# A three-stack transformer kernel: columns for the first norm's weights, halves for the first unit and for the output, products of zeros at the start

## The chip, the cores and the metric

The kernel runs on one core of one Trainium2 chip. A core has five engines with instruction queues of their own: TensorE (PE) for matrix products, VectorE (DVE), ScalarE (ACT), GpSimd (POOL), and SyncE (SP), which here issues DMA transfers. The metric is device time in microseconds for one execution, the median of several runs; before the change it is 2333.55 us (three runs, 2333.11 to 2333.55).

## The reference

The input is 512 tokens of width 1024 in float32. Two hybrid layers follow (dilated attention, mLSTM, gated mixing, a feed-forward part), a norm, then a second block of two layers (latent attention and gated linear attention, with a context of 256 tokens) and a last norm. What the change touches is the first operation and the last two:

```
def rms_norm(x, w):
    xf = x.astype(jnp.float32)
    y = xf * lax.rsqrt(jnp.mean(xf * xf, axis=-1, keepdims=True) + NORM_EPS)
    return (y * w.astype(jnp.float32)).astype(x.dtype)

h = rms_norm(x, norm_mix_w)      # first layer: the first thing that is computed
z = h @ w_in + b_in              # the first columns of z are the queries
...
x = x + gx * yx                  # second block, second layer: the last projection
return rms_norm(x, final_g)      # the output, (1, 512, 1024)
```

## The kernel before, in words

Tokens lie in four tiles of 128 partitions, `xs[0]` to `xs[3]`, each 128x1024. Weights come from memory in units of 128x1024 (512 KB) in the order in which they are used; `P.stream` gives a function `W` that hands out the next unit. A product in float32 is made of three products in the faster type float32r: every operand `v` is held as a high part (`v` rounded, made by ACT, line 251) and a low part (`v` less its high part, made by DVE, line 252). `split` makes the two, `mm3` (lines 280 to 282) issues high by high, high by low and low by high into one PSUM bank. `wide_acc` does eight steps of `mm3` for one token tile over four units: 24 products with 512 columns.

At the start SP issues, in this order, tile x0, the identity, the norm's weights `wbc` (one row of 4 KB repeated over 128 partitions, line 221), units 0 and 1, x1, units 2 and 3, x2, x3, and then small tables. `Norm` takes one tile at a time: ACT squares it with a running sum (line 298), DVE makes the mean (289), POOL the power -1/2 (291), DVE multiplies by that number and by the row of weights in one pass (300), PE transposes the eight 128x128 blocks into two PSUM banks (757), and each bank is split by one ACT and one DVE instruction into `big`, the stationary operand of the products. Between tile 0 and tile 1 the program asks for the first four units, so their splits stand there. The Q projection then runs over the four tiles (line 414 adds the bias and frees the bank), followed by K, V and the rest.

The unit's raw landing place has two slots (four for the first units, in `land`), the split unit has four. A slot is loaded again when its split is done, and a split unit is overwritten when the products that read it are done.

At the end `output(1)` of `gla` goes through tiles and, for each, two halves `ch` of 512 columns: 12 products, DVE times the gate (1574), DVE adds to `xs[t]` (1575). After the second half `rms` squares the whole tile on ACT, makes the mean and the power, scales it in one DVE pass of 1024 columns (300), and SP stores 512 KB (1578). Two PSUM banks `A` take turns there.

The order of instructions on each engine is settled when the kernel is built: a planner goes through the program with its own estimates of durations and gives each engine, whenever it is free, the earliest instruction in program order that is ready by them. On the chip each engine keeps that order. Lines 973 and 974, in another class (`Tokens.put`), split transposed blocks one by one with a number per partition, much as the changed kernel does in its first norm.

Of the kernel before, what the change touches and what calls it, by code (L numbers as in the profile page):

```python
# [25 lines left out]
C_AQ, C_AK, C_AV, C_MQ, C_MK, C_MV, C_MO = (512 * i for i in range(7))  # L26
C_MI = 3584
C_GA, C_GB = 3592, 4616
QUARTERS = ((0, 0), (0, 1), (1, 1), (1, 0))


# [13 lines left out]
def _cols(v):  # L45

    return v.reshape(-1, 128).T
# [116 lines left out]
def layout(a):  # L164
    m = {}
    for l in range(2):
        m[f"wl{l}"] = pack_layer(a, l)
        m[f"wq{l}"] = pack_quarters(a, l)
        m[f"cl{l}"] = pack_cols(a, l)
        m[f"wg{l}"] = np.ascontiguousarray(_tall(a["w_in"][l], C_MI, 8))  # L170
    m["x"] = a["x"].reshape(S, D)
    m["pos"] = np.ascontiguousarray(a["positions"].reshape(4, 128).T)
    for k in ("b_in", "norm_mix_w", "norm_mlp_w"):
        m[k] = a[k]
    m["mla"], m["gla"], m["gla_g"] = pack_mla(a), pack_gla(a), pack_gates(a)
    m["gla_b"] = np.concatenate([_cols(a["gla_b_gb_2"][0]), _cols(a["gla_b_gf_2"][0])], axis=1)
    m["gla_o_norm"] = a["gla_o_norm_2"]
    m["mla_q_norm"], m["mla_kv_norm"] = a["mla_q_norm_2"], a["mla_kv_norm_2"]
    for i in range(2):
        m[f"ada{i}"] = a["ada_w_2"][i].T.reshape(24, 128, 1024)  # L180
    m["ada_b"] = np.stack([_cols(a["ada_b_2"][i]) for i in range(2)], axis=1)
    m["cvec"] = np.concatenate([a["c_2"].reshape(-1), a["c_ctx_2"].reshape(-1)])
    m["norm_g"] = np.stack([_cols(a["norm_g_2"][i]) for i in range(2)])
    m["final_g"] = a["final_g_2"].reshape(1, D)
    m["ctx"] = a["ctx_2"].reshape(256, D)
    m["final_norm_w"] = a["final_norm_w"].reshape(1, D)
    m.update({"k_" + k: v for k, v in constants().items()})
    return {k: np.ascontiguousarray(v) for k, v in m.items()}
# [8 lines left out]
class Prog:  # L197
# [59 lines left out]
    def stream(self, key):  # L257
        units = self.A[key]
        state = {"i": 0}
        ahead = []  # L260

        def fetch(n=1024, raw=None):
            raw = self.raw.tile([128, 1024], F32, name="raw") if raw is None else raw
            self.nc.sync.dma_start(raw[:, 0:n], units[state["i"]][:, 0:n])
            state["i"] += 1
            ahead.append(raw)

        def nxt(n=1024):
            if not ahead:
                fetch(n)  # L270
            raw = ahead.pop(0)
            w = self.spl.tile([128, 2, 1024], F32R, name="spl")
            self.split(w[:, 0, 0:n], w[:, 1, 0:n], raw[:, 0:n])
            return w
        nxt.state, nxt.fetch = state, fetch
        return nxt
# [26 lines left out]
def act_of(tiles):  # L303

    return lambda k: (tiles[k // 4][:, 0, k % 4], tiles[k // 4][:, 1, k % 4])


def cut(a):

    return lambda t, k: tuple(v[:, t * 128:(t + 1) * 128] for v in a(k))  # L310
# [31 lines left out]
def first_block(P, xs, pool):  # L342
# [6 lines left out]
    for l in range(2):  # L349
# [9 lines left out]
        if l == 0:  # L359
            def load_x(t):  # L360
                nc.sync.dma_start(xs[t], A["x"][t * 128:(t + 1) * 128])
            load_x(0)
            P.ident = P.load(P.const, "k_ident", [128, 128], "ident")
            norm = Norm(P, xs, A["norm_mix_w"][0], one, tmp, big)
            land = big(3, F32).rearrange("p a k n -> p (a k n)").rearrange("p (i n) -> p i n", i=4)
            for i in (0, 1):
                W.fetch(raw=land[:, i])
            load_x(1)
            for i in (2, 3):
                W.fetch(raw=land[:, i])  # L370
            for t in (2, 3):
                load_x(t)
            for t in range(4):
                norm(t)()
                if t == 0:
                    first += [W() for _ in range(4)]
            mod = Modulation(P)
            dil = P.load(ck, "k_dil", [128, 512], "dil")
            anti = P.load(ck, "k_anti", [128, 128], "anti")
            pair = P.load(ck, "k_pair", [128, 5], "pair")  # L380
            pair_r = ck.tile([128, 4], F32R, name="pair_r")
            nc.scalar.activation(pair_r, pair[:, 0:4], AF.Copy)
# [356 lines left out]
class Norm:  # L739
# [7 lines left out]
    def __call__(self, t):  # L747

        P = self.P
        xn = self.tmp.tile([128, 1024], F32, name="xn", tag="qm")  # L750
        rms(P, xn, self.xs[t], self.wbc, xn)

        def later():
            for g in range(2):
                ps = P.bankT()
                for k in range(4):
                    P.nc.tensor.transpose(ps[:, k * 128:(k + 1) * 128], xn[:, (4 * g + k) * 128:(4 * g + k + 1) * 128],
                                          P.ident)
                o = slice(t * 128, (t + 1) * 128)
                P.split(self.dst[g][:, 0, :, o], self.dst[g][:, 1, :, o], ps.rearrange("p (k n) -> p k n", k=4))  # L760
        return later


# [538 lines left out]
def gla(P, xs, finish, keep, mod, out):  # L1302
# [246 lines left out]
    def output(kh):  # L1549
        sg = gate[0]  # L1550
        if kh == 0:
            output.G = right.tile([128, 1024], F32, name="G", tag="qk0")
            gate_row(P, output.G, mod, 0)
        G = output.G
        oT = left.tile([128, 2, 4, 512], F32R, name="oT", tag=f"hx{kh}")
        for h in (2 * kh, 2 * kh + 1):
            v = sg[:, :, h * 256:(h + 1) * 256]
            nc.vector.tensor_tensor(v, v, held[h], op=OP.mult)
        for t in range(4):
            ps = P.bankT()  # L1560
            for k in range(4):
                nc.tensor.transpose(ps[:, k * 128:(k + 1) * 128], sg[:, t, (4 * kh + k) * 128:(4 * kh + k + 1) * 128], P.ident)
            d = oT[:, :, :, t * 128:(t + 1) * 128]
            P.split(d[:, 0], d[:, 1], ps.rearrange("p (k n) -> p k n", k=4))
        yield
        a, us = cut(act_of([oT])), {}
        order = [(ch, t) for ch in range(2) for t in range(4)]
        for ch, t in [(ch, t) for t in range(4) for ch in range(2)] if kh else order:
            if ch not in us:
                us[ch] = [W() for _ in range(2)]  # L1570
            c = slice(ch * 512, (ch + 1) * 512)
            ps = P.bankA()
            wide_acc(P, ps, us[ch], a, t, 4)
            nc.vector.tensor_tensor(ps, ps, G[:, c], op=OP.mult)
            nc.vector.tensor_tensor(xs[t][:, c], xs[t][:, c], ps, op=OP.add)
            if kh and ch:
                rms(P, xs[t], xs[t], row, right.tile([128, 1024], F32, name="sq", tag=f"qk{2 + t % 2}"))
                nc.sync.dma_start(out[t * 128:(t + 1) * 128], xs[t])
            yield


# [38 lines left out]
```

## Time and profile before

| what | value |
|---|---|
| median of three runs | 2333.55 us |
| the profiled execution's own time | 2335.07 us |
| its span, first to last instruction | 2333.3 us |
| PE busy | 2284.1 us, 98% |
| DVE busy | 1478.0 us, 63% |
| ACT busy | 1063.0 us, 46% |
| granted clock of PE, mean | 0.998 |

All times in rows are microseconds from the span's start unless marked ns. `PE` is the product, `PEld` the load of its stationary operand, which overlaps the product before. An idle time in brackets is that of the engine just before the row, with what ended it. A matrix product's duration covers its way through the array, so the spacing of the starts, or the chain of waits, tells what one costs in a run of them.

### The profile page before, as it was taken

The numbers are of one execution on the slowest core, as the hardware profiler recorded it, in microseconds if no ns is written. First come the engines' busy times: TensorE is split into PE (matmuls) and PEld (weight loads), VectorE is DVE, ScalarE is ACT, GpSimd is POOL, SyncE is SP. The second block draws the span as 40 slices with busy tenths as digits, with TensorE's granted clock in tenths as the row PEclk, the third lists the DMA queues.
The fourth block names the chain that finished last, engine by engine and source line by source line (L and its number), as shares of the span: only waits on it lengthen the run. The fifth ranks groups of instructions, "written<-read, shape, count | busy, mean of one in ns | idle before, by whom it ended". The sixth has DMA issues, their size and how long they took to land.

```text
span 2333.3 us, 30784 instructions
## 1 busy us (share of the span) xinstructions
PE 2284.1 (98%) x12108; PEld 1875.9 (80%) x12108; DVE 1478.0 (63%) x2556; ACT 1063.0 (46%) x1958; POOL 71.4 (3%) x120
## 2 busy tenths in 40 slices
PE   8999999999999999999999999999999999999998
PEld 6777878888888777788888888888888888788886
DVE  4477796555555547779645556564478776756586
ACT  3366423444443235642344445452477772563332
POOL 0000000000000000000000000010000000000000
PEclk9999999999999999999999999999999999999999
DMA  4221464555642322146454554212110121121112
GB/s 162 81 73 55 145 212 142 167 130 151 174 100 91 92 81 75 52 155 216 135 172 120 160 164 116 92 54 72 49 31 21 24 74 37 54 81 37 55 46 72
DMA packets 61312, 234.38 MB, mean 100 GB/s; under 512 B 8544, under 2 KB 9840, under 8 KB 54768
## 3 DMA queue, kind: packets, MB, share of 16 engines
q1 hardware_dynamic: 50512, 179.99, 23.3%
q0 software_dynamic: 3456, 25.17, 6.0%
q10 hardware_dynamic: 7200, 27.27, 3.7%
q8 instruction: 95, 1.56, 0.3%
q14 instruction: 49, 0.40, 0.1%
HBM read 227.15 MB, written 2.10 MB: 98 GB/s over the span
## 4 chain that ended last, share of the span: by engine, by line
PE 81%; DVE 10%; ACT 3%; DMA 3%; issue 2%; POOL 1%; SPq 0%; POOLq 0%; ACTq 0%; DVEq 0%
PE A L282 18%; PE A L281 18%; PE A L280 18%; PE S L280 4%; PE S L282 4%; PE S L281 4%; PE O L1244 2%; DVE spl L252 2%; PE T L1236 2%; PE O L522 1%; DMA ada<-in_ada 1%; PE S L496 1%; DVE junk L933 1%; PE T L516 1%; ACT spl L251 1%
## 5 line engine op out<-in xcount | busy, mean ns | idle before, releaser
L280 PE MATMUL A<-big,spl 128*128 128x512 f32 (+1 forms) x1280 | 482.2, 377 | 1.9 <-DVE x L768 1.2
L282 PE MATMUL A<-big,spl 128*128 128x512 f32 (+1 forms) x1280 | 481.0, 376 | 0.2 <-DVE spl L252 0.2
L281 PE MATMUL A<-big,spl 128*128 128x512 f32 (+1 forms) x1280 | 480.1, 375 | 0.0
L252 DVE TENSOR_TENSOR spl<-raw,spl 128x1024 fp32r<-128x1024 f32 (+2 forms) x265 | 317.2, 1200 | 184.0 <-ACT spl L251 182.2
L251 ACT ACTIVATE spl<-raw 128x1024 fp32r<-128x1024 f32 (+2 forms) x265 | 275.2, 1040 | 292.2 <-PE A L282 190.6
L282 PEld LDWEIGHTS A<-big,spl 128*128 128x128 f32 x1280 | 241.2, 188 | 44.6 <-issue 2.6
L280 PEld LDWEIGHTS A<-big,spl 128*128 128x128 f32 x1280 | 241.3, 189 | 43.9 <-DVE x L768 1.6
L281 PEld LDWEIGHTS A<-big,spl 128*128 128x128 f32 x1280 | 241.3, 189 | 42.5 <-issue 1.4
L252 DVE TENSOR_TENSOR spl<-quarter,spl 128x1024 fp32r<-128x1024 f32 x84 | 102.2, 1223 | 144.9 <-ACT spl L251 144.9
L280 PE MATMUL A<-spl,big 128*128 128x512 f32 (+2 forms) x480 | 182.7, 384 | 3.7 <-DVE tg L668 2.1
L281 PE MATMUL A<-spl,big 128*128 128x512 f32 (+2 forms) x480 | 182.3, 381 | 1.4 <-DVE spl L252 0.8
L282 PE MATMUL A<-spl,big 128*128 128x512 f32 (+2 forms) x480 | 181.7, 380 | 0.2 <-DVE ms L289 0.2
L251 ACT ACTIVATE spl<-quarter 128x1024 fp32r<-128x1024 f32 x84 | 88.2, 1057 | 97.4 <-PE S L282 41.1
L280 PEld LDWEIGHTS A<-spl,big 128*128 128x128 f32 x480 | 90.2, 189 | 23.2 <-DVE tg L668 3.0
L281 PEld LDWEIGHTS A<-spl,big 128*128 128x128 f32 x480 | 90.7, 189 | 18.9 <-DVE spl L252 3.4
L282 PEld LDWEIGHTS A<-spl,big 128*128 128x128 f32 x480 | 90.6, 189 | 16.7 <-issue 1.1
L280 PE MATMUL S<-spl,part 128*128 128x512 f32 x264 | 102.8, 389 | 0.0
L281 PE MATMUL S<-spl,part 128*128 128x512 f32 x264 | 102.8, 389 | 0.0
L282 PE MATMUL S<-spl,part 128*128 128x512 f32 x264 | 102.8, 389 | 0.0
L1211 DVE TENSOR_REDUCE mx<-S 128x1 f32<-128x768 f32 (+1 forms) x80 | 71.8, 900 | 26.5 <-PE S L282 25.7
L291 POOL TENSOR_TENSOR rstd<-ms,mhalf 128x1 f32<-128x1 f32 (+2 forms) x68 | 44.2, 650 | 1247.5 <-DVE ms L289 1203.2
L1237 ACT ACTIVATE pt<-T 128x512 f32<-128x512 f32 (+1 forms) x144 | 66.4, 501 | 32.4 <-PE T L1236 31.2
(442 smaller groups left out, 4349.2 us busy)
## 6 DMA issues: line engine op xcount, KB each, us to landing
raw<-in_wl SPq DMA_DIRECT2D x196, 512.0 KB, 3.7
ada<-in_ada ACTq DMA_DIRECT2D x48, 512.0 KB, 4.0
quarter<-in_wq SPq DMA_DIRECT2D x24, 1024.0 KB, 6.2
quarter<-in_wq POOLq DMA_DIRECT2D x24, 1024.0 KB, 8.7
raw<-in_gla SPq DMA_DIRECT2D x33, 512.0 KB, 3.4
raw<-in_mla SPq DMA_DIRECT2D x20, 512.0 KB, 3.5
raw<-in_mla SPq DMA_DIRECT2D x8, 384.0 KB, 3.0
qT<-rot SPq DMA_DIRECT2D x32, 96.0 KB, 2.8
```

What stands on the lines that cost most here:

```text
L251: nc.scalar.activation(hi, src, AF.Copy)
L252: nc.vector.tensor_tensor(lo, src, f32(hi), op=OP.subtract)
L280: mm(ps, lh, rh, start=start, stop=False, **more)
L281: mm(ps, lh, rl, start=False, stop=False, **more)
L282: mm(ps, ll, rh, start=False, stop=stop, **more)
L291: nc.gpsimd.tensor_tensor(r, ms, self.mhalf[:, 0:w], op=OP.pow)
L496: nc.tensor.matmul(banks[hh][:, 0:w], qT[hs, i, q], kT[hs, j, 0:w], start=(i + j == 0), stop=(i == 1))
L516: nc.tensor.transpose(psp[:, k * 128:(k + 1) * 128], p[:, k * 128:(k + 1) * 128], P.ident)
L1211: nc.vector.tensor_reduce(mx[:, 0:two], pss[:, 0:two * m].rearrange("p (t n) -> p t n", t=two), AX.X, OP.max, negate=True)
L1236: nc.tensor.transpose(pst[:, k:k + 128], p[:, o + k:o + k + 128], P.ident)
L1237: nc.scalar.activation(pt[:, o:o + w], pst[:, 0:w], AF.Copy)
L1244: nc.tensor.matmul(weigh.o[64 * i:64 * i + 64, (t0 + t) * 128:(t0 + t + 1) * 128], V[4 * c + k][:, h * 64:(h + 1) * 64], pts[i][:, t * m + ...
```

## The change

Four edits. (1) The weights of the first layer's first norm are laid out as 128x8 columns, `first_w` (4 KB), and a new class `FirstNorm` takes the place of `Norm` there: DVE multiplies the tile by its number alone, and the weight of each transposed block of 128 features is applied in the split, as the scale of ACT's copy and of DVE's pass, eight of each per tile. (2) Unit 0 is loaded in two transfers of 256 KB and split in two halves. (3) A tile of zeros and 14 products of it (128x128 by 128x512) into one PSUM bank stand ahead of the first norm; nothing reads their result. (4) In the last stage the tile's square is taken in two halves as they are finished, the mean is put together in two DVE steps, and the scaled tile is made and stored in two halves.

```
--- before.py
+++ after.py
@@ -26,6 +26,7 @@
 C_AQ, C_AK, C_AV, C_MQ, C_MK, C_MV, C_MO = (512 * i for i in range(7))
 C_MI = 3584
 C_GA, C_GB = 3592, 4616
+WARM = 14
 QUARTERS = ((0, 0), (0, 1), (1, 1), (1, 0))
 
 
@@ -169,6 +170,7 @@
         m[f"cl{l}"] = pack_cols(a, l)
         m[f"wg{l}"] = np.ascontiguousarray(_tall(a["w_in"][l], C_MI, 8))
     m["x"] = a["x"].reshape(S, D)
+    m["first_w"] = np.ascontiguousarray(_cols(a["norm_mix_w"][0]))
     m["pos"] = np.ascontiguousarray(a["positions"].reshape(4, 128).T)
     for k in ("b_in", "norm_mix_w", "norm_mlp_w"):
         m[k] = a[k]
@@ -259,18 +261,21 @@
         state = {"i": 0}
         ahead = []
 
-        def fetch(n=1024, raw=None):
+        def fetch(n=1024, raw=None, cut=1):
             raw = self.raw.tile([128, 1024], F32, name="raw") if raw is None else raw
-            self.nc.sync.dma_start(raw[:, 0:n], units[state["i"]][:, 0:n])
+            for o in range(0, n, n // cut):
+                self.nc.sync.dma_start(raw[:, o:o + n // cut], units[state["i"]][:, o:o + n // cut])
             state["i"] += 1
             ahead.append(raw)
 
-        def nxt(n=1024):
+        def nxt(n=1024, cut=1):
             if not ahead:
                 fetch(n)
             raw = ahead.pop(0)
             w = self.spl.tile([128, 2, 1024], F32R, name="spl")
-            self.split(w[:, 0, 0:n], w[:, 1, 0:n], raw[:, 0:n])
+            for o in range(0, n, n // cut):
+                c = slice(o, o + n // cut)
+                self.split(w[:, 0, c], w[:, 1, c], raw[:, c])
             return w
         nxt.state, nxt.fetch = state, fetch
         return nxt
@@ -361,19 +366,25 @@
                 nc.sync.dma_start(xs[t], A["x"][t * 128:(t + 1) * 128])
             load_x(0)
             P.ident = P.load(P.const, "k_ident", [128, 128], "ident")
-            norm = Norm(P, xs, A["norm_mix_w"][0], one, tmp, big)
+            norm = FirstNorm(P, xs, one, tmp, big)
             land = big(3, F32).rearrange("p a k n -> p (a k n)").rearrange("p (i n) -> p i n", i=4)
             for i in (0, 1):
-                W.fetch(raw=land[:, i])
+                W.fetch(raw=land[:, i], cut=2 - i)
             load_x(1)
             for i in (2, 3):
                 W.fetch(raw=land[:, i])
             for t in (2, 3):
                 load_x(t)
+
+            nil = tmp.tile([128, 512], F32R, name="nil", tag="yf")
+            nc.vector.tensor_copy(nil, P.zero.to_broadcast([128, 512]))
+            idle = P.bankO()
+            for i in range(WARM):
+                nc.tensor.matmul(idle, nil[:, 0:128], nil, start=(i == 0), stop=(i == WARM - 1))
             for t in range(4):
                 norm(t)()
                 if t == 0:
-                    first += [W() for _ in range(4)]
+                    first += [W(cut=2 - (i > 0)) for i in range(4)]
             mod = Modulation(P)
             dil = P.load(ck, "k_dil", [128, 512], "dil")
             anti = P.load(ck, "k_anti", [128, 128], "anti")
@@ -761,6 +772,35 @@
         return later
 
 
+class FirstNorm:
+
+
+    def __init__(self, P, xs, one, tmp, big):
+        self.col = P.load(one, "first_w", [128, 8], "first_w")
+        self.dst = [big(i) for i in range(2)]
+        self.P, self.xs, self.tmp = P, xs, tmp
+
+    def __call__(self, t):
+        P, nc = self.P, self.P.nc
+        xn = self.tmp.tile([128, 1024], F32, name="xn", tag="qm")
+        ssq = P.sm.tile([128, 1], F32, name="ssq")
+        nc.scalar.activation(xn, self.xs[t], AF.Square, accum_out=ssq)
+        r = P.rstd(ssq, D)
+        nc.vector.tensor_scalar(xn, self.xs[t], r, None, op0=OP.mult)
+
+        def later():
+            o = slice(t * 128, (t + 1) * 128)
+            for g in range(2):
+                ps = P.bankT()
+                for k in range(4):
+                    v, c = ps[:, k * 128:(k + 1) * 128], 4 * g + k
+                    nc.tensor.transpose(v, xn[:, c * 128:(c + 1) * 128], P.ident)
+                for k in range(4):
+                    v, c = ps[:, k * 128:(k + 1) * 128], 4 * g + k
+                    P.split(self.dst[g][:, 0, k, o], self.dst[g][:, 1, k, o], v, scale=self.col[:, c:c + 1])
+        return later
+
+
 def add_wide(P, W, a, xs, scale, done=None):
 
     def evac(ch, t, ps):
@@ -1564,6 +1604,9 @@
             P.split(d[:, 0], d[:, 1], ps.rearrange("p (k n) -> p k n", k=4))
         yield
         a, us = cut(act_of([oT])), {}
+        if kh:
+            eps = P.sm.tile([128, 1], F32, name="eps")
+            nc.gpsimd.memset(eps, EPS)
         order = [(ch, t) for ch in range(2) for t in range(4)]
         for ch, t in [(ch, t) for t in range(4) for ch in range(2)] if kh else order:
             if ch not in us:
@@ -1573,9 +1616,22 @@
             wide_acc(P, ps, us[ch], a, t, 4)
             nc.vector.tensor_tensor(ps, ps, G[:, c], op=OP.mult)
             nc.vector.tensor_tensor(xs[t][:, c], xs[t][:, c], ps, op=OP.add)
-            if kh and ch:
-                rms(P, xs[t], xs[t], row, right.tile([128, 1024], F32, name="sq", tag=f"qk{2 + t % 2}"))
-                nc.sync.dma_start(out[t * 128:(t + 1) * 128], xs[t])
+            if kh:
+
+                if not ch:
+                    sq = right.tile([128, 1024], F32, name="sq", tag=f"qk{2 + t % 2}")
+                ssq = P.sm.tile([128, 1], F32, name="ssq")
+                nc.scalar.activation(sq[:, c], xs[t][:, c], AF.Square, accum_out=ssq)
+                ms = P.sm.tile([128, 1], F32, name="ms")
+                nc.vector.scalar_tensor_tensor(ms, ssq, 1.0 / D, part if ch else eps, op0=OP.mult, op1=OP.add)
+                part = ms
+                if ch:
+                    r = P.sm.tile([128, 1], F32, name="rstd")
+                    nc.gpsimd.tensor_tensor(r, ms, P.mhalf[:, 0:1], op=OP.pow)
+                    for i in range(2):
+                        h = slice(512 * i, 512 * i + 512)
+                        nc.vector.scalar_tensor_tensor(xs[t][:, h], xs[t][:, h], r, row[:, h], op0=OP.mult, op1=OP.mult)
+                        nc.sync.dma_start(out[t * 128:(t + 1) * 128, h], xs[t][:, h])
             yield
 
 
```

## Rows read from the trace of the kernel before

**Rows 1.** The page, section 1: busy time, share of the span, instructions.

```profile
PE 2284.1 (98%) x12108; PEld 1875.9 (80%) x12108; DVE 1478.0 (63%) x2556; ACT 1063.0 (46%) x1958; POOL 71.4 (3%) x120
```

**Rows 2.** Waits of the first 60 us: who waited for whom, total, times, longest.

```profile
ACT spl L251 <- DMA big<-in_wl: 4.7, 2, 4.5
...
DVE xn L300 <- DMA wbc<-in_norm_mix_w: 3.1, 1, 3.1
```

**Rows 3.** Timeline of the first 62 us: start, duration, engine, line, operation.

```profile
4.25 1.06 ACT L298 ACTIVATE xn<-x 128x1024 f32<-128x1024 f32 x1 [2.24 <-DMA x<-in_x]
...
5.74 0.55 POOL L291 TENSOR_TENSOR rstd<-ms,mhalf 128x1 f32<-128x1 f32 x1 [4.76 <-DVE ms L289]
...
8.73 1.28 DVE L300 SCALAR_TENSOR_TENSOR xn<-x,rstd,wbc 128x1024 f32<-128x1024 f32 x1 [3.14 <-DMA wbc<-in_norm_mix_w]
...
12.79 0.79 PE L280 MATMUL A<-spl,big 128*128 128x512 f32 x1 [0.75 <-ACT big L251]
...
40.39 0.69 DVE L414 TENSOR_TENSOR big<-A,bias 128x512 f32<-128x512 f32 x1 [0.35 <-PE A L282]
```

**Rows 4.** Chain that ended last, first 60 us: start, duration, what.

```profile
16.24 0.43 PE A L280
...
18.46 0.44 PE T L757 x4
...
28.09 0.23 PE A L280
```

**Rows 5.** Waits of SP's queue, first 30 us.

```profile
SPq L215 <- DMA wbc<-in_norm_mix_w: 1.6, 1, 1.6
```

**Rows 6.** Timeline of SP's queue, first 70 us.

```profile
8.61 0.33 SPq L215 DMA_DIRECT2D ada_b<-in_ada_b  x1
...
17.53 0.33 SPq L215 DMA_DIRECT2D inv<-in_k_inv  x1
```

**Rows 7.** Groups by line and form: count, busy us, mean ns, idle before.

```profile
L251 ACT ACTIVATE big<-T 128x512 fp32r<-128x512 f32 x32 | 18.1, 593 | 16.0 <-PE T L757 15.8
L973 ACT ACTIVATE big<-T,mod 128x128 fp32r<-128x128 f32 x48 | 16.0, 365 | 10.9 <-DVE big L974 7.1 <-PE T L969 3.3
...
L974 DVE SCALAR_TENSOR_TENSOR big<-T,mod,big 128x128 fp32r<-128x128 f32 x48 | 15.1, 344 | 2.1 <-ACT big L973 1.6
L504 DVE TENSOR_SCALAR p<-p,sl 128x512 f32<-128x512 f32 x16 | 7.8, 485 | 0.4
L252 DVE TENSOR_TENSOR spl<-big,spl 128x1024 fp32r<-128x1024 f32 x4 | 4.8, 1221 | 1.0 <-ACT spl L251 1.0
```

**Rows 8.** Timeline of ACT and DVE, 2017 to 2019: lines 973 and 974.

```profile
2017.56 0.60 DVE L974 SCALAR_TENSOR_TENSOR hx<-T,mod,hx 128x128 fp32r<-128x128 f32 x2
2017.94 0.62 ACT L973 ACTIVATE hx<-T,mod 128x128 fp32r<-128x128 f32 x2 [1.48 <-DVE hx L974]
2018.34 0.61 DVE L974 SCALAR_TENSOR_TENSOR hx<-T,mod,hx 128x128 fp32r<-128x128 f32 x2 [0.18 <-ACT hx L973]
```

**Rows 9.** Timeline of the end, 2324 to 2330.

```profile
2324.82 0.70 DVE L1574 TENSOR_TENSOR A<-A,G 128x512 f32<-128x512 f32 x1 [0.21 <-PE A L282]
...
2326.33 1.06 ACT L298 ACTIVATE sq<-x 128x1024 f32<-128x1024 f32 x1 [4.51 <-DVE x L1575]
...
2327.81 0.55 POOL L291 TENSOR_TENSOR rstd<-ms,mhalf 128x1 f32<-128x1 f32 x1 [5.12 <-DVE ms L289]
2328.39 1.28 DVE L300 SCALAR_TENSOR_TENSOR x<-x,rstd,frow 128x1024 f32<-128x1024 f32 x1 [0.73 <-POOL rstd L291]
```

**Rows 10.** DMA issues, 2328 to 2334: count, KB each, us to landing.

```profile
out<-x SPq DMA_DIRECT2D x1, 512.0 KB, 2.6
```

**Rows 11.** Timeline of PE in the output stage, 2313 to 2314.

```profile
2313.41 0.47 PE L280 MATMUL A<-spl,oT 128*128 128x512 f32 x1 [0.16 <-DVE x L1575]
```

**Rows 12.** Busy us of each engine by stretch, granted clock (PEclk), DMA share, GB/s.

```profile
2024.90:2028.40 3.50, 1.97 (x11) 1.44 (x12) 2.22 (x7) 3.09 (x10) 0.00 (x0) 1.00 0.35 135
2028.40:2031.80 3.40, 3.40 (x12) 2.72 (x11) 1.99 (x7) 2.53 (x8) 0.00 (x0) 0.50 0.00 0
```

## The prediction

> **What bounds the kernel now.** I read the page first. TensorE (PE) is busy 98% of the span [rows 1], so only time in which PE waits or runs slowly is worth anything, and outside the middle that is two stretches: before the first product and after the last. Then the waits of the first 60 us: VectorE (DVE) waits 3.1 us for `wbc`, the 512 KB row of the norm's weights, before it can scale tile 0, and ScalarE (ACT) waits 4.7 us for the first weight units [rows 2]. The timeline shows what hangs on them: x0 is squared at 4.25, its rstd is ready by 6.29, yet tile 0 is scaled only at 8.73, and the first product of the Q projection starts at 12.79 [rows 3]. The chain of waits then shows two sizes of step: 0.43 us a product at 16.2, 0.23 at 28.1 [rows 4]. These are the two levels of PE's clock, 1.2 and 2.4 GHz; before 18 us PE is at the lower one. The group ends when DVE takes its last bank at 40.39 [rows 3].
>
> How much of 12.79 to 40.35 is work? 96 products of 0.227 (0.23 in the chain) are 21.8 us, and 24 transposes of 0.11 (four in 0.44) [rows 4] are 2.6, together 24.4 of 27.6. The other 3.2 us are low clock and waits: between 12.79 and 18 PE does about 2.7 us worth of full-speed work, so 2.5 of the 3.2 lie there.
>
> **The loads.** After its tenth load SP issues each further one only when an earlier one has landed; `ada_b` goes out when `wbc` has landed, at 8.61, and seven loads later `inv` at 17.53 [rows 5, 6]. So each 512 KB takes 1.27 us, and unit 0 lands near 9.9, unit 1 at 11.2, x1 12.4, units 2 and 3 at 13.7 and 14.9, x2 and x3 at 16.2 and 17.5. But `wbc` itself lands 4.3 us after x0 is in use at 4.25, though only 64 KB stand between: it costs about 4 us, not 1.27 (128 reads of the same 4 KB row). The change puts 4 KB of columns in its place. Bounds for what all later loads gain: 1.27 (its bytes) to 4.4; I take 4.4, since the slot from 4.25 to 8.61 holds nothing else. The columns are 128 rows of 32 B; no row shows such a load alone, so between nothing and 0.6 us (half a 512 KB load); I take 0.2, which leaves 4.2. Unit 0 then comes in two halves near 5.1 and 5.7, unit 1 at 7.0, x1 8.2, unit 2 9.5, unit 3 10.7, x2 12.0, x3 13.3. (With 1.27 alone units 2 and 3 come 2.9 later and hold tile 0 up by some 1.5, inside the bounds of the sum below.) SP issues one DMA more ahead of loads that wait for the queue anyway: nothing.
>
> **The first scaled tile.** The chain x0, square, mean, rstd is unchanged to 6.29. The scaling loses its row operand: 1.28 us before [rows 3], now a multiply by one scalar; 512 columns of that take 0.485 [rows 7], so 0.49 to 1.28 for 1024, and I take 0.75 by the gap to the two-operand form. DVE has the low part of unit 0's first half (about half of 1.22) in front, so xn is ready at 7.4 instead of 10.0. Transposes end near 8.3 at the high clock, 9.0 at the low. ACT converts both halves of unit 0 (0.6 each) by 6.6 and unit 1 by 8.05. First product: 8.7 (8.0 if the splits come at once, 10.3 if the transposes are cold and ACT does unit 2 first). That is 4.1 us earlier.
>
> **The split by columns.** This is the cost. Before, a bank of four transposed blocks took one ACT of 0.59 and one DVE pass; now it takes four of each, with the weight column as scale. The same form runs at line 973/974: 0.365 on ACT, 0.344 on DVE [rows 7], in pairs 0.78 us apart (2017.56 to 2018.34), each ACT pair starting only when the first DVE of the pair before has ended [rows 8]. Eight pieces a tile are thus 3.4 us in a row, against some 1.9; in engine time about 2.0 on ACT (1.2 before) and 2.1 on DVE (1.4 before). PE needs 24 products and 8 transposes a tile, 6.3 us, so tiles 1 to 3 are covered. Tile 0 is not: after 8.05 DVE has three low parts of 1.22 [rows 7], eight pieces (2.1) and tile 1's scaling with its mean (0.9), 6.7 us, and idles perhaps 0.8 for ACT: it feeds the last piece of tile 0 at 15.5. From 8.7 PE alone would finish tile 0 and tile 1's transposes at 15.1. I charge 1.0 for this, 0.5 for waits as in the later part of the group before (0.7), and nothing for the clock.
>
> **The zeros.** One DVE copy and 14 products with N=512, from about 1.6 us. At 0.43 each [rows 4] they end at 7.6, at 0.23 from some point earlier; PE has nothing else until 7.5, so they hide. If they raise the clock, the 2.5 us found above shrink to what I charged. No row shows a product of zeros, so the bounds are nothing and 2.5.
>
> **Sum of the start.** 8.7 + 24.4 + 1.5 = 34.6 against 40.35: 5.7 us. Bounds: 10.3 + 24.4 + 3.2 = 37.9 (2.4 gained) and 8.0 + 24.4 + 0.5 = 32.9 (7.4). What is late next: the units of the K projection, whose slots come free with these products, so they move along.
>
> **The output.** After the last product the chain is two DVE passes, a square of 1.06 at 2326.33, a mean, rstd at 2327.81, a scaling of 1.28 at 2328.39, and a store of 512 KB that lands 2.6 us after its issue [rows 9, 10]. The square over half the columns is about 0.6 (0.59 for 512 [rows 7]): minus 0.45. The scaling in two halves ends 0.1 later, but the second store has half the bytes: minus 0.6 of the 1.27 (bounds 0 and 0.64). The first half's store is issued 0.65 earlier and is over before. Together 1.0, bounds 0.3 and 1.1. Extra small work (a square, a mean step a tile) lies beside 5.4 us of products. One place is open: before, the 1.28 scaling stands in front of DVE's add, and PE restarts only when that frees its bank (2313.41) [rows 11]. Two scalings of 0.68 can stand there as well or let the add pass between: minus 0.4 to plus 0.4; I take 0.
>
> **Total.** 5.7 + 1.0 = 6.7. The span of 2333.3 becomes 2326.6; the profiled execution's own 2335.07 (1.77 around the span) becomes 2328.4, and it stands 1.52 above the median of the runs, 2333.55, which becomes 2326.9. A measurement here can tell about 0.2%, 4.7 us, from no change: the limits are 2328.9 and 2338.2.
>
> **Rivals.**
> A, the forecast: 2326.9; own range 2325.2 to 2328.9.
> B, the split paces tiles 0 and 1. ACT keeps its order and stands behind pieces that wait for DVE, which is in a 1.22 us low part: three times about 0.9 is 2.7 us more. For it: the ACT wait of 1.48 in rows 8; against: PE has other tiles' transposes to fill with. 4.0 gained, 2329.5.
> C, the clock. Zeros might not raise it, or it falls again before real products are dense. The trace has such falls: with PE busy 1.97 of 3.5 us to 2028.4, the granted clock is 0.50 in the next 3.4 us, the lower level [rows 12]. Between 7.6 and 10 PE would have only transposes and products paced by splits, which is like that. Loss 2.3, so 4.4 gained, 2329.2. The Trainium skill (TensorE: Matmul & The Clock Gate, section on HAM oscillation) says that too thin a burst followed by a wait puts the array back to half clock each time; the trace agrees with its 0.50, and by that rule the sum would be C's.
> D, the gain of the start is given back at a later load, and only the output's 1.0 stays: 2332.5. For it: ACT waits for weights early on [rows 2]; against: later loads are issued when a slot comes free, not at a fixed time.
> E, slower. The order of work on each engine is planned anew when the kernel is built, and a start that ends 6 us earlier can change it far behind. Place and price: a stretch like that of rows 12, in which PE idles 1.5 of 3.5 us and then runs 3.4 us at half clock, costs 3.2. Three new ones, 9.6, outweigh the 6.7: 2336.5. For it: the plan does leave such a hole there; against: PE's work, which the plan follows, is the same from 40 us on.
> One stretch more or less, or a fall of the clock by itself (1.7), may come in every case.
>
> **How the numbers follow.** A 0.62, B 0.14, C 0.12, D 0.07, E 0.05. Below 2328.9 lie nine tenths of A and a third of B and C: faster 0.65; slower than 2338.2 needs four such stretches: 0.03, and 0.04 with what no case names; same 0.31. The range 2324.8 to 2331.0 holds A, B and C but for their ends, and leaves out D and E.
>
> **What would show it.** Right: no load of 512 KB ahead of unit 0; first real product near 8.7, at 0.23 a step from the start; last bank of the Q group taken near 34.6; from DVE's first pass after the last product to the end of the span 7.5 instead of 8.5. Wrong: steps of 0.43 after 9 us (C); PE idle before tile 1 with ACT waiting for DVE at the split (B); a shift of 6 us at 40 that is gone by 100 or 1000 (D).

## The result, and the profile after

The changed kernel is slower by 1.2%: 2360.82 us (median of four runs, 2360.48 to 2361.63) against 2333.38 for the kernel before on the same chip; ratio 1.0118, 95% interval 1.0101 to 1.0136. The prediction was 2326.9. The profiled execution of the changed kernel took 2360.78, its span 2358.8. Here and below a ratio compares the undisturbed runs of both kernels, so it can differ a little from the quotient of the two medians.

The page, section 1, of the changed kernel, answers to [rows 1]:

```profile
PE 2320.4 (98%) x12122; PEld 1876.4 (80%) x12122; DVE 1483.8 (63%) x2590; ACT 1070.6 (45%) x1991; POOL 71.4 (3%) x121
```

PE is busy 36.3 us longer for 14 products more, and the 14 are the zeros, 5.1 us. So 31 us lie in the same products as before. The groups by line and form (count, busy us, mean ns, idle before) show them a little longer each. Before, and then after:

```profile
L280 PE MATMUL A<-big,spl 128*128 128x512 f32 x1088 | 427.1, 393 | 0.2
...
L281 PE MATMUL A<-big,spl 128*128 128x512 f32 x1088 | 425.6, 391 | 0.0
```

```profile
L285 PE MATMUL A<-big,spl 128*128 128x512 f32 x1088 | 432.0, 397 | 0.2
...
L286 PE MATMUL A<-big,spl 128*128 128x512 f32 x1088 | 430.9, 396 | 0.0
```

A mean contains the way through the array. The distance between the starts of two neighbouring products of 512 columns, taken from some 6,960 pairs, is 0.2278 us on average before and 0.2329 after (medians 0.227 and 0.232), with the clock fully granted in both. The start of the n-th product, transposes counted too, from 0, and zeros left out, shows when the time is lost:

```
product       10     130     800    2000    3200    4400    5600    6800    8000   12107
before     14.16   40.64  179.36  425.65  676.78  932.52 1178.24 1428.95 1655.63 2324.39
after      11.87   40.02  180.27  429.14  685.96  946.52 1195.11 1452.00 1681.51 2350.44
shift      -2.29   -0.63   +0.91   +3.49   +9.18  +14.00  +16.87  +23.05  +25.88  +26.05
```

The loss creeps in up to about product 8000; a single stall would be one jump. The longer steps explain its size. Behind product 800 they make an estimated 33 us (0.0052 by some 6,370 steps). TensorE (PE) then idles 5.6 us less, as the next two rows show (stretch less PE busy: 26.8 us before, 21.2 after; columns as in [rows 12]). And the kernel before has two falls of the clock there (at 2028.4 and 2110.3), the changed one only one (at 2052.9), which is worth 1.7. That leaves 25.7, against 25.1 in the table.

```profile
179.36:2324.39 2145.03, 2118.20 (x11310) 1750.81 (x11308) 1374.10 (x2349) 984.26 (x1806) 66.51 (x101) 1.00 0.33 100
```

```profile
180.27:2350.44 2170.17, 2148.93 (x11310) 1750.20 (x11308) 1376.87 (x2354) 985.45 (x1812) 66.48 (x101) 1.00 0.33 99
```

From product 8000 on the loss stands still: only some 1,240 steps of 512 columns lie there, 3.5 us in all, and the missing fall and 1.7 us less idle time take that up.

The start, in the timeline of the changed kernel (columns as in [rows 3]):

```profile
1.38 5.12 PE L383 MATMUL O<-nil 128*128 128x512 f32 x14 [1.38 <-DVE nil L380]
...
4.32 1.06 ACT L787 ACTIVATE xn<-x 128x1024 f32<-128x1024 f32 x1 [2.30 <-DMA x<-in_x]
...
6.45 0.63 ACT L253 ACTIVATE spl<-big 128x512 fp32r<-128x512 f32 x1 [0.98 <-DMA big<-in_wl]
7.76 0.63 ACT L253 ACTIVATE spl<-big 128x512 fp32r<-128x512 f32 x1 [0.69 <-DMA big<-in_wl]
...
8.43 0.69 DVE L254 TENSOR_TENSOR spl<-big,spl 128x512 fp32r<-128x512 f32 x1 [0.62 <-ACT spl L253]
9.04 0.74 DVE L789 TENSOR_SCALAR xn<-x,rstd 128x1024 f32<-128x1024 f32 x1
9.24 1.06 ACT L253 ACTIVATE spl<-big 128x1024 fp32r<-128x1024 f32 x1 [0.84 <-DMA big<-in_wl]
...
10.95 0.50 PE L285 MATMUL A<-spl,big 128*128 128x512 f32 x1
11.29 0.39 PE L286 MATMUL A<-spl,big 128*128 128x512 f32 x1
11.87 0.51 PE L287 MATMUL A<-spl,big 128*128 128x512 f32 x1 [0.20 <-DVE big L257]
...
13.46 1.22 DVE L254 TENSOR_TENSOR spl<-big,spl 128x1024 fp32r<-128x1024 f32 x1
13.73 0.50 PE L285 MATMUL A<-spl,big 128*128 128x512 f32 x1 [0.50 <-ACT big L256]
...
15.00 0.49 PE L287 MATMUL A<-spl,big 128*128 128x512 f32 x1 [0.54 <-DVE big L257]
15.12 1.22 DVE L254 TENSOR_TENSOR spl<-big,spl 128x1024 fp32r<-128x1024 f32 x1
...
16.65 0.65 PE L797 MATMUL T<-ident,xn 128*128 128x128 f32 x4 [0.52 <-DVE big L257]
...
39.75 0.69 DVE L425 TENSOR_TENSOR big<-A,bias 128x512 f32<-128x512 f32 x1 [0.43 <-PE A L287]
```

The first real product starts at 10.95 (12.79 before), already at the high clock, and the last Q bank (the last PSUM bank of the Q projection) is taken at 39.75 (40.39 before), against 8.7 and 34.6 predicted. The end (columns as before; [rows 9] are its counterpart):

```profile
2350.87 0.70 DVE L1617 TENSOR_TENSOR A<-A,G 128x512 f32<-128x512 f32 x1
2351.74 0.16 DVE L1626 SCALAR_TENSOR_TENSOR ms<-ssq,eps 128x1 f32<-128x1 f32 x1 [0.17 <-ACT sq L1624]
2351.82 0.68 DVE L1618 TENSOR_TENSOR x<-x,A 128x512 f32<-128x512 f32 x1
...
2352.53 0.63 ACT L1624 ACTIVATE sq<-x 128x512 f32<-128x512 f32 x1 [0.82 <-DVE x L1618]
...
2354.17 1.41 DVE L1633 SCALAR_TENSOR_TENSOR x<-x,rstd,frow 128x512 f32<-128x512 f32 x2 [0.73 <-POOL rstd L1630]
```

From 2350.87 to the end of the span are 7.93 us, against 8.48 before.

### The profile page after: what moved, and what is told of

The parts are those of the page before. It is cut to its first block, busy times and chain, and to the rows that moved or that the text cites. A ratio compares the mean times of both kernels' runs of the same rounds, so it can differ in the third digit from the quotient of the medians.

```text
span 2358.8 us, 30886 instructions
## 1 busy us (share of the span) xinstructions
PE 2320.4 (98%) x12122; PEld 1876.4 (80%) x12122; DVE 1483.8 (63%) x2590; ACT 1070.6 (45%) x1991; POOL 71.4 (3%) x121
## 4 chain that ended last, share of the span: by engine, by line
PE 85%; DVE 8%; ACT 3%; issue 2%; DMA 2%; POOL 1%; SPq 0%; DVEq 0%; POOLq 0%; ACTq 0%
PE A L287 19%; PE A L286 19%; PE A L285 19%; PE S L285 4%; PE S L286 4%; PE S L287 4%; PE O L1284 2%; PE T L1276 2%; DVE spl L254 2%; PE O L533 1%; PE S L507 1%; PE T L527 1%; PE O L286 1%; PE O L287 1%; PE O L285 1%
## 5 line engine op out<-in xcount | busy, mean ns | idle before, releaser
L285 PE MATMUL A<-big,spl 128*128 128x512 f32 (+1 forms) x1280 | 487.1, 381 | 1.7 <-DVE x L808 1.0
L287 PE MATMUL A<-big,spl 128*128 128x512 f32 (+1 forms) x1280 | 486.1, 380 | 0.2 <-DVE spl L254 0.2
L286 PE MATMUL A<-big,spl 128*128 128x512 f32 (+1 forms) x1280 | 485.1, 379 | 0.0
```

The source lines that it names most:

```text
L285: mm(ps, lh, rh, start=start, stop=False, **more)
L286: mm(ps, lh, rl, start=False, stop=False, **more)
L287: mm(ps, ll, rh, start=False, stop=stop, **more)
```

## The experiments

A look at where the tiles lie gave the theory. `eps`, a 4-byte tile per partition, is a new name in the pool `sm`, which has four slots of 32 bytes per name: 128 bytes. The pool lies between the split weights `spl` and nearly everything else on that side, so `big` moved from 36608, a multiple of 256, to 36736, while `spl` stayed at 2304, a multiple too. Theory: the place of a product's operands decides its step. Rivals: the zeros, the new order of work, the new code.

Kernels of one set ran on one chip, beside runs of the kernel before. The runs of one kernel spread over some 5 us here, partly because the granted clock falls for 3.4 us at different places in different executions (as in [rows 12]); so what is worth 1 or 2 us is read from the traces, not from medians.

**First set.** The change without `eps`:

```
-            eps = P.sm.tile([128, 1], F32, name="eps")
-            nc.gpsimd.memset(eps, EPS)
...
-                nc.vector.scalar_tensor_tensor(ms, ssq, 1.0 / D, part if ch else eps, op0=OP.mult, op1=OP.add)
+                if ch:
+                    nc.vector.scalar_tensor_tensor(ms, ssq, 1.0 / D, part, op0=OP.mult, op1=OP.add)
+                else:
+                    nc.vector.tensor_scalar(ms, ssq, 1.0 / D, EPS, op0=OP.mult, op1=OP.add)
```

> The changed kernel, except that the mean's first half gets its epsilon as a constant of the instruction (one multiply-and-add of the same size) and the 128x1 tile that held it is gone, so that every later tile of the left side lies where it lay before the change. Address theory: the product step returns from 0.232 to 0.227 us in all stages, and what is left is the wanted part of the change: about 0.9 us gained at the start and 0.5 at the end, 2331 to 2333 us. Zeros theory (the products of zeros or the early clock leave PE slower for the whole run): step 0.232, 2360. Code theory (28 more PE instructions shift its instruction stream): step 0.232, 2360.

The kernel before with an unused tile in `eps`'s place, of 1, 16 or 32 numbers per partition (128, 256 and 512 bytes in the pool's four slots):

```
+            pad = P.sm.tile([128, 1], F32, name="pad")     # or [128, 16], [128, 32]
+            nc.gpsimd.memset(pad, EPS)
```

> The kernel before with one unused 128x1 tile (one memset) in the pool of small tiles, where the changed kernel has its epsilon: 4 slots of 32 bytes, all later tiles of the left side move by 128 bytes. Nothing else of the change. Address theory: step 0.232 in the products of weight units and activations, 2359 to 2362 us. Zeros theory and code theory: 2333 to 2334, step 0.227.

> The same with a pad of 256 bytes (4 slots of 64). Address theory, with 512 bytes as the distance that counts (the products of hi and lo with weight units, 256 bytes off, already step by 0.233 in the kernel before): 0.233, 2358 to 2364 us. With 256 bytes as the distance: 2333 to 2334. Zeros and code theories: 2333 to 2334.

> The same with a pad of 512 bytes (4 slots of 128). Address theory: the distance between the two operands of a product is again a multiple of 512 bytes, step 0.227, 2333 to 2334 us. If any move of the tiles costs time, 2360. Zeros and code theories: 2333 to 2334.

Measured (before: 2333.3): without `eps` 2332.70, ratio 0.9995 (0.9986 to 1.0004); 128 bytes 2362.44, ratio 1.0123 (1.0109 to 1.0137); 256 bytes 2332.82, 0.9999 (0.9990 to 1.0008); 512 bytes 2332.56, 0.9997 (0.9988 to 1.0006). The mean step is 0.2277 to 0.2278 in all but the kernel with 128, which has 0.2329. So an unused tile alone makes the whole loss, and without it the change loses nothing. Zeros, order and code are out: the kernel with 128 bytes has only one memset of them, which those with 256 and 512 have too. The groups by line and form of the kernels with 128 and with 256 bytes:

```profile
L280 PE MATMUL A<-big,spl 128*128 128x512 f32 x1088 | 432.1, 397 | 0.2
```

```profile
L280 PE MATMUL A<-big,spl 128*128 128x512 f32 x1088 | 426.6, 392 | 0.2
```

**Is it the address, or the distance between the two operands?** The kernel before with 128 bytes ahead of `spl`, so that weights and activations move together; and with 64 bytes between them:

```
+        pad = self.const.tile([128, 32], F32, name="pad")                       # ahead of spl: 128
+        pad = self.pool("pad", 1).tile([128, 16], F32, name="pad")              # behind sm: 64
```

> The kernel before with 128 bytes more in the first pool, ahead of the split weights: weights and activations both lie 128 bytes further, so their distance is unchanged, and each is 128 bytes off a multiple of 256. If the address itself decides (theory), the products step at about 0.231 to 0.233 us and the time is 2356 to 2363 us. If only the distance between the two operands decides (rival), the step stays 0.228 and the time 2333.

> The kernel before with 64 bytes between the split weights and the activations. If every distance that is no multiple of 256 bytes is slow: step 0.232 to 0.234, 2358 to 2364 us, as with 128. If only 128 (or an odd number of 32) is slow: step 0.228, 2333.

Measured: moved together 2333.07 against 2333.01, ratio 0.9998 (0.9989 to 1.0007), mean step 0.2279; 64 between them 2356.10 against 2332.55, ratio 1.0099 (1.0085 to 1.0113), mean step 0.2317. The same group, moved together and then 64 apart:

```profile
L282 PE MATMUL A<-big,spl 128*128 128x512 f32 x1088 | 426.6, 392 | 0.2
```

```profile
L282 PE MATMUL A<-big,spl 128*128 128x512 f32 x1088 | 430.9, 396 | 0.3
```

My theory of the address falls; the rival, the distance, holds: both operands may lie 128 off, so long as they lie there alike. With 64 between them the direction counts too: products with `big` as moving operand, 64 past the stationary `spl`, step at 0.230, and those with `spl` moving and `big` stationary at 0.233.

**The products that were slow all along.** The latent attention's `cqT`, `hi`, `lo` and `V` lie 224 past a multiple of 256 in the kernel before (the expectation for 256 bytes had put `hi` and `lo` 256 off), the identity 192. Pads bring them in line, once on the change without `eps`, once on the kernel before:

```
+            pad  = P.const.tile([128, 16], F32, name="pad")    # ahead of the identity: 64
+            pad2 = P.const.tile([128, 48], F32, name="pad2")   # behind it: 192
+    pad_r = right.tile([128, 56], F32, name="pad_r")           # under cqT: 224
```

> The change without the extra tile, and two pads that bring the latent attention's operands (cqT, hi, lo, V) and the identity, which lay 224 and 192 past a multiple of 256 in every kernel so far, onto a multiple. Theory of the address: 336 products of 512 columns, about 6.5 ns less each, are 2.2 us, and 108 of 256 columns some 0.3; the 900 products of 128 columns may give 0 to 4 more. So 2327 to 2330.5 where the change without the tile is 2332.7. Rival (those steps are slow for another reason): 2332.7, and the steps at hi, lo and cqT stay at 0.233.

> The kernel before, with only the pads that bring the identity, cqT, hi, lo and V onto the same place modulo 256 bytes as the operands that they meet; nothing of the change is in it. If the pads alone make what the padded change gained beyond the unpadded one: 2.5 to 4.5 us below the kernel before, 2329 to 2331, and some 1 us above the padded change. If the padded change was faster for its shorter start and output: 2333, the same as before.

Measured: on the change 2328.37 against 2333.01, ratio 0.9983 (0.9974 to 0.9992); on the kernel before 2331.23 against 2332.55, ratio 0.9995 (0.9986 to 1.0004). The steps at `hi` and `lo`, 0.233 to 0.234 before, are 0.226 to 0.227 in both; those at `cqT` fall only from 0.233 to 0.229. This is the group of `hi` on the change, without pads and with them:

```profile
L286 PE MATMUL A<-spl,hi 128*128 128x512 f32 x96 | 38.0, 396 | 0.0
```

```profile
L286 PE MATMUL A<-spl,hi 128*128 128x512 f32 x96 | 37.5, 390 | 0.0
```

The padded change is the only version whose interval lies below the kernel before, by 0.17%. Some 2 us of that should be the pads (6,960 steps at 0.2278 less as many at 0.2275, the new mean), but the kernel with the pads alone can't be told from none, so the split between pads and change is an estimate, not measured.

**The start and the output.** Three kernels on the change without `eps` or its padded form: without the zeros, with the output as before, with unit 0 whole; a fourth loads the columns behind units 0 and 1:

```
# no zeros
-            for i in range(WARM):
-                nc.tensor.matmul(idle, nil[:, 0:128], nil, start=(i == 0), stop=(i == WARM - 1))
# output as before
-                ssq = P.sm.tile([128, 1], F32, name="ssq")
...
+            if kh and ch:
+                rms(P, xs[t], xs[t], row, right.tile([128, 1024], F32, name="sq", tag=f"qk{2 + t % 2}"))
# unit 0 whole
-                W.fetch(raw=land[:, i], cut=2 - i)
+                W.fetch(raw=land[:, i])
...
-                    first += [W(cut=2 - (i > 0)) for i in range(4)]
+                    first += [W() for _ in range(4)]
# columns behind unit 1
-        self.col = P.load(one, "first_w", [128, 8], "first_w")
+            norm.col = P.load(one, "first_w", [128, 8], "first_w")
```

> The change without the extra tile and without the products of zeros. If the zeros keep the clock up through the start: the first products go at 0.43 us a step and the time is about 1.5 to 2.5 us above that of the change without the tile, 2334 to 2335. If the start is paced by the splits whatever the clock is: 2332.7, no difference, and the step of the first products at the low clock lies inside the waits.

> Only the start of the change (columns, halves of unit 0, zeros), the output as before. If the output's halves gain the 1.0 us that the prediction gave them, this is 1.0 above the change without the tile: 2333.7. If their gain is 0.5 as the trace of the changed kernel has it: 2333.2. If the order planned for the last stage costs something: below 2332.7.

> The padded change with unit 0 in one transfer and one split. If the second half's transfer and low part are what holds tile 0's scaling back: the whole unit lands where its second half did (7.5 us), its low part of 1.2 stands ahead of the scaling, and the scaling starts 0.5 later, near 9.3 instead of 8.8. If the planned order puts the scaling first: it starts at 6.4 to 6.6, and the first product comes 2 us earlier, near 8.7. The whole time moves by less than a single run can tell.

> The padded change with the 4 KB of weight columns loaded behind units 0 and 1 instead of ahead of them. If that small load of 128 rows of 32 B holds the queue: ACT takes the first half of unit 0 at about 5.0 instead of 6.0. If only bytes count (the queue moved about 2 MB by 8.5 us with the row of weights and without it): at 6.0 as before.

Without zeros 2331.68, ratio 0.9998 (0.9989 to 1.0007); with the output as before 2331.51, ratio 0.9995 (0.9985 to 1.0004); both against 2333.01, so no difference that the runs can tell. (The second lies below all three times expected of it, but that doesn't show the third case, a cost of the planned order.) In the trace without zeros the first products do go at the low clock, 0.43 to 0.59 apart, yet PE has caught up soon: its product or transpose number 30, counted as above, starts at 18.29, in the changed kernel at 18.92 and in that without `eps` at 18.13.

```profile
11.22 0.80 PE L285 MATMUL A<-spl,big 128*128 128x512 f32 x1
11.81 0.63 PE L286 MATMUL A<-spl,big 128*128 128x512 f32 x1
12.24 0.63 PE L287 MATMUL A<-spl,big 128*128 128x512 f32 x1
```

Its last Q bank is taken at 39.07, with the zeros and without `eps` at 38.63, and with zeros and pads at 39.61: the zeros' worth is inside that spread. What PE waits for between its first product and that bank (total us, times, longest) shows why. First the changed kernel, then the one without zeros:

```profile
PE A L287 <- DVE big L257: 0.7, 2, 0.5
PE T L797 <- DVE big L257: 0.7, 2, 0.5
PE A L285 <- ACT big L256: 0.5, 1, 0.5
```

```profile
PE A L287 <- DVE big L257: 0.2, 1, 0.2
```

At the low clock PE waits less for the splits, and the group ends at about the same time.

The last two kernels are compared with the padded change, whose rows come first below. With unit 0 whole (one run, 2329.89), ACT takes it at 6.62 and the scaling starts at 8.85, against 6.01 and 8.80 with halves. That is neither expectation (9.3, or 6.5): the whole unit is in use 0.9 before the second half was (7.53), and its copy of 1.06 and low part of 1.23 take that back. With the columns later (one run, 2327.39) ACT takes unit 0's first half at 6.28, not at 5.0. So the small load holds up nothing that shows beside landings which move by up to 1 us between executions.

```profile
6.01 0.63 ACT L253 ACTIVATE spl<-big 128x512 fp32r<-128x512 f32 x1 [0.67 <-DMA big<-in_wl]
...
7.53 0.63 ACT L253 ACTIVATE spl<-big 128x512 fp32r<-128x512 f32 x1 [0.89 <-DMA big<-in_wl]
...
8.80 0.75 DVE L793 TENSOR_SCALAR xn<-x,rstd 128x1024 f32<-128x1024 f32 x1
```

```profile
6.62 1.06 ACT L253 ACTIVATE spl<-big 128x1024 fp32r<-128x1024 f32 x1 [1.30 <-DMA big<-in_wl]
...
7.71 1.23 DVE L254 TENSOR_TENSOR spl<-big,spl 128x1024 fp32r<-128x1024 f32 x1 [2.20 <-ACT spl L253]
8.85 0.75 DVE L793 TENSOR_SCALAR xn<-x,rstd 128x1024 f32<-128x1024 f32 x1
```

```profile
6.28 1.32 ACT L253 ACTIVATE spl<-big 128x512 fp32r<-128x512 f32 x2 [1.20 <-DMA big<-in_wl]
```

## Why the prediction was wrong, point by point

**The step that failed** is in the paragraph on the output: "Extra small work (a square, a mean step a tile) lies beside 5.4 us of products." It priced the new instructions and not the new tile. With it goes the silent term that the middle of the span stays as it is: the sum has only the start and the output, as if every product between them would cost what it had cost. `eps` cost no time of its own, but 128 bytes of place, and with them 0.005 us on each of some thousands of products: +26 us at the last product. The 128-byte pad alone shows it: 2362.44, and 2332.70 for the change without `eps`. Rival E, the slower one, named the planned order as its mechanism and is wrong too: no case held this, and the chance of slower was 0.04. Nothing in the profile of before points to it but one thing that I passed over: its products at `hi`, `lo` and `cqT` already had steps of 0.233 beside 0.227 elsewhere.

Without `eps` the change is about even (0.6 us faster by the medians, and between 3.3 faster and 0.9 slower by the interval), where 6.7 was forecast. So the rest was wrong as well, by some 6 us.

**The loads: 4.2 predicted, 1.8 found**, the bound of bytes alone being 1.27. (In the four other traces with unit 0 in halves and the columns ahead of it, the load `inv` goes out 1.7 to 2.7 earlier than before.) I read the slot from 4.25 to 8.61 as `wbc`'s own. The rate row of the DMA view (GB/s in slices of 0.5 us, first 20 us), before and then after, says otherwise:

```profile
GB/s 0 0 0 90 287 360 367 280 214 221 156 197 303 393 393 393 410 393 426 426 418 434 393 426 426 418 434 393 426 375 374 250 222 215 195 91 55 61 98 270
```

```profile
GB/s 0 0 0 41 254 295 404 244 204 217 303 344 311 303 324 377 377 385 401 418 434 418 401 434 426 418 401 397 347 289 312 205 107 58 165 229 418 336 360 418
```

The first 17 slices hold 2.03 MB before and 2.00 after. Before, only x0, the identity and `wbc`, together 1.11 MB, were in use by then: units 0 and 1 were on their way beside `wbc`. So the row of weights did not hold the queue for 4 us. The gain lies nearer to its bytes; what makes it more than 1.27 stays open. SP's queue after shows the later loads 1.8 earlier (17.53 in [rows 6]), landings moving by up to 1 us between executions:

```profile
9.23 0.33 SPq L217 DMA_DIRECT2D anti<-in_k_anti  x1
...
15.71 0.33 SPq L217 DMA_DIRECT2D inv<-in_k_inv  x1
```

**The scaled tile: 7.4 predicted to be ready, 9.8 found.** The multiply's 0.75 was right (0.74). DVE keeps its planned order, in which both low parts of unit 0's halves stand ahead of the scaling, and ACT can take the second half only at 7.76. I had put one low part there. (Without `eps` the order is the same, but ACT takes both halves in a row from 5.96 on, and the tile is ready at 8.6.) The rstd was ready by 6.4. First product 10.95: the 2.25 us over 8.7 come from this and the loads.

**The split by columns**: pieces of 0.37 and 0.34, as priced, but the pace is rival B's. In the timeline above PE waits for a piece at 13.73, 15.00 and 16.65, while DVE is in the 1.22 low parts of 13.46 and 15.12. From the first product to the last Q bank are 28.8 us, 2.9 more than the 24.4 + 1.5 that I allowed: 0.5 is the longer step (96 by 0.005), so 2.4 are left, which I put down to B, priced at 2.7. The waits shown above for this stretch are 1.9, more than the 1.5 allowed.

**The zeros** raise the clock, as hoped: in the changed kernel the second real product starts 0.34 after the first, in the kernel without zeros 0.59. They gain nothing that can be seen, because the splits set the pace. Rival C nevertheless happened in three of the six traced kernels with zeros: without `eps`, with the output as before, and with unit 0 whole, where the second product comes after 0.57 to 0.59 again. Here are the stretches of the first (columns as in [rows 12]), then the stretch after the fall in each of the two others, and then those of the changed kernel:

```profile
5.50:9.00 3.50, 1.56 (x8) 0.99 (x7) 1.98 (x3) 1.80 (x3) 0.53 (x1) 0.97 0.94 355
9.00:12.40 3.40, 3.40 (x14) 2.74 (x12) 2.58 (x6) 3.17 (x7) 0.56 (x1) 0.53 1.03 423
```

```profile
10.60:14.00 3.40, 3.40 (x11) 2.07 (x10) 2.88 (x7) 3.40 (x9) 0.55 (x1) 0.50 1.03 409
```

```profile
9.60:13.00 3.40, 3.34 (x12) 2.99 (x13) 2.99 (x6) 2.95 (x7) 0.56 (x1) 0.50 1.03 417
```

```profile
5.50:9.00 3.50, 1.00 (x5) 0.48 (x3) 1.42 (x3) 1.26 (x2) 0.55 (x1) 1.00 0.94 346
9.00:12.40 3.40, 2.35 (x12) 1.47 (x13) 2.57 (x6) 2.93 (x7) 0.20 (x1) 1.00 1.03 419
```

The changed kernel idled more and kept the clock, the one without `eps` lost it (0.53), and the one that lost it took its last Q bank earlier. Nor does the wait between the zeros and the first transposes tell them apart: 3.34 us in the changed kernel, 1.94 in the one without `eps`. The rule of the Trainium skill that the prediction quoted (TensorE: Matmul & The Clock Gate, section on HAM oscillation) is about a burst of products that is shorter than the wait behind it. The zeros here take 5.0 to 6.2 us and the waits behind them 1.5 to 3.3, so these traces don't test it.

**The sum of the start**: 34.6 + 2.25 + 2.4 + 0.5 = 39.75, where the bank was taken: 0.6 gained instead of 5.7. The 2.4 is the remainder, so the sum had to come out. In the other kernels with zeros the bank is taken between 38.60 and 39.76.

**The output: 1.0 predicted, 0.55 found** (8.48 less 7.93). The second store gave 0.4 instead of 0.6 (from the scaling's end to the end of the span 3.63 before, 3.22 after). The square's half gave 0.27 instead of 0.45, because the first half's mean step (2351.74) stands between the two last passes and starts the square 0.15 later. The scaling in halves cost 0.13, as said. In the runs this can't be told: the kernel with the output as before is as fast as the others.

**D** (the start's gain given back) can't be judged in the changed kernel, where the creep covers it. Without `eps` the last Q bank is 1.8 earlier and the products 5600 and 8000 are 2.2 earlier: up to there nothing was given back.

## What to carry to other kernels

A new tile has a price beside its instructions: where the pools are laid end to end, look at what moves behind it, and compare the addresses modulo 256 of the two operands of the products that fill the span. A wait that ends with a load does not say that the queue worked for that load alone; add up what moved against what had landed. A clock that is raised ahead of time is worth only what the next limit leaves, here the splits.

## What the runs showed of the hardware

A 128x128 by 128x512 product in float32r, in a run of such products, steps at 0.227 us (median) where its moving and its stationary operand start at the same place modulo 256 bytes, and slower where not (counted from the stationary operand to the moving one, modulo 256): 0.230 where the moving one lies 64 past the stationary one and 0.233 where it lies 192 past it (the kernel with 64 bytes between), 0.232 at 128, 0.233 to 0.234 at 32 and 0.232 to 0.233 at 224 (`hi`, `lo` and `cqT` in the kernel before), 0.232 at 96 (`cqT`) and 0.234 to 0.235 at 160 (`hi`, `lo`) with `spl` and `big` moved together. Moving both by 128 leaves it at 0.227; with 256 or 512 bytes between them it is 0.227. Over this kernel that is 1.0 to 1.2% of the time.

The Trainium skill (SBUF — State Buffer, section "Who interferes with whom") gives PE two independent read ports, one for the moving operand and one for the weight load, and says that PE never waits on anyone. The runs don't agree with independent: the distance between the two sets the step. Why is open; a meeting of the two reads in the memory would fit, but no run looked for it. Two things do not fit the simple rule. The products of `kT` with `qT` in the latent attention, whose operands lie alike in all these kernels, have steps from 0.225 to 0.240; by tile their medians are 0.227 to 0.231 in the kernel before and 0.227 to 0.235 in the change without `eps`, where every address is as before. And the products of zeros, whose two operands start at the very same address, stepped at 0.228 to 0.236 in the changed kernel once the clock was up.
